# First feed-forward matrix by seven half-size products, second matrix in chunks, in a hybrid encoder layer

## Chip, cores and metric

The kernel runs on one core of one Trainium2 chip. The metric is the device time of one launch in microseconds (us), median of the runs. The engines of a core are named as in the profile: PE (TensorE, matrix products; PEld is its loading of weights), DVE (VectorE), ACT (ScalarE), POOL (GpSimd), SP (SyncE, which issues most DMAs).

## The reference, cut to what matters

One layer, 512 tokens and 16 meta tokens, 1024 features, float32. The layer is feed forward, mixer, feed forward, each with a norm ahead and behind it:

```
def swiglu(x, wi, wo):                 # wi: 1024 x 5632, wo: 2816 x 1024
    a, b = split(x @ wi, 2)
    return (silu(a) * b) @ wo

h = h + 0.5 * rmsnorm(swiglu(rmsnorm(h, n[0]), ffn1_wi, ffn1_wo), n[1])
h = h + rmsnorm(hybrid_mixer(rmsnorm(h, n[2]), ...), n[3])
h = h + 0.5 * rmsnorm(swiglu(rmsnorm(h, n[4]), ffn2_wi, ffn2_wo), n[5])
return h[16:]
```

The first feed forward has all 528 token columns, the second only the 512 that are returned. The mixer is not touched by the change.

## The kernel before

**Layout.** Features lie on partitions, tokens on columns: `hT` is [128, 8, 528]. A weight matrix is stored as tiles of 128 output features, each [128, 8, 128] for 1024 inputs (512 KB). `wi` has 44 of them: tiles 0 to 21 are `a`, tiles 22 to 43 are `b`, so that tile m and tile 22+m make a pair (`KF` is 22). `wo` has 8 tiles (`KD`), each of 22 inner tiles.

**Exact products.** Every float32 operand is split into two float32r parts of 12 significand bits, `h` and `l`: ACT casts (L219, L224), DVE subtracts what the cast kept (L220, L225). `mm` (L227) makes a product from three passes: h by h, h by l, l by h. `load` (L212) stages a weight tile in `ws` (2 buffers), splits it to `wh` and `wl` (3 buffers each), and asks for a priority that lies 150 instructions ahead (`AHEAD`). Only PE's order is written by hand; the other engines' orders come from a scheduler that goes by priority, which otherwise is the order in the program. Each engine then runs its own queue in order.

**A unit** (`unit`, L243) is one tile of `wi` against all columns: 8 inner tiles by 3 passes. For the first feed forward the 528 columns go as two halves of 264 in two PSUM banks, 48 matrix instructions (`ALLC`); for the second as one bank of 512, 24 instructions (`REAL`). There are two PSUM pools of four banks each, `pb` (`big`) and `pd` (`dnp`).

**Feed forward** (`ffn`, L518). The norm ahead of it is applied late: the products use h times the gain, and the factor `rx` (one per token, written by the reciprocal at L276) multiplies what comes out (`scaled`, L502; L539, L542 for the first pairs). Per pair: two units, scale, silu, multiply (L526), split into `gh` and `gl`, which hold all 22 inner tiles. The first three units come with the pre-stage (`start` L334, or `edge` L375); the next three run while `rx` is made. Then the second matrix: for output tile m = 0 to 6 all 22 inner tiles are summed in PSUM (L557 to L563), and `evict_y` (L305) copies the result to `y`, squares it and sums the squares in `acc`. Tile 7 is the tail.

**Tail, edge and finish.** The last output tiles are made for one half of the columns and then for the other (`part`, L324), so that the norm of the first half can start under the products of the second. `edge` (L375) goes from one stage to the next, `finish` (L431) writes the output: DVE multiplies and adds 8 tiles of the first half (L461, L462), PE transposes, and after the last product ACT squares it (L489) and DVE makes the last rows (L499). For the feed forwards the tail is one tile with 22 inner tiles; for the mixer it is three tiles with 8.

Of the kernel before, what the change touches and what calls it, by code (L numbers as in the profile page):

```python
# [29 lines left out]
AHEAD = 150  # L30
XW = 5.0
# [23 lines left out]
# columns of the packed constants  # L55
# [45 lines left out]
class Cols:  # L101
    """Token columns of a stage, in two halves; joined: both fit one PSUM bank."""
# [17 lines left out]
class Tensor:  # L120
    """The tensor engine's instructions, with a sum of their length that orders the side work."""
# [22 lines left out]
class K:  # L144
# [43 lines left out]
    # side work goes between the large products; it yields how far on its next part goes  # L188
# [22 lines left out]
    # weights: staged as stored, then split into two parts of 12 significand bits  # L211
# [93 lines left out]
    def evict_y(self, ya, m, ps, gain=None, table=KD - 2):  # L305
        """ps: (half, what the products of tile m gave for it)"""
        y, acc = ya
        ACT, V = self.nc.scalar, self.nc.vector
        for i, p in ps:
            w = acc[i].shape[1]  # L310
            if gain is None:
                ACT.copy(y[i][:, m, :w], p)
            else:
                ACT.activation(y[i][:, m, :w], p, AF.Copy, scale=self.gains[:, gain, m:m + 1])
            if m == 0:
                ACT.activation(acc[i], p, AF.Square)
            else:
                sq = self.t(self.tp, "sy", [P, HN], F32, 1)[:, :w]
                ACT.activation(sq, p, AF.Square)  # L319
                V.tensor_tensor(acc[i], acc[i], sq, op=ALU.add)  # L320
        if m == table:
# [12 lines left out]
    def start(self, xT, gpre, srcs):  # L334
        """the first norm and tiles: everything arrives in the order of need"""
# [28 lines left out]
        # warm-up products while the first loads arrive  # L364
# [10 lines left out]
    def edge(self, C, hT, ya, gpost, gpre, tail, switch, nxt):  # L375
# [18 lines left out]
        tiles, tx, tc = tail()  # L394
        for t in tiles:
            self.evict_y(ya, t[0], [(0, self.part(t, tx, tc[0], W))], table=tiles[0][0] - 1)
# [12 lines left out]
        for t in tiles:  # L409
            self.evict_y(ya, t[0], [(1, self.part(t, tx, tc[1], W, lambda: next(e, None)))], table=-1)  # L410
# [20 lines left out]
    def finish(self, hT, ya, tail, out):  # L431
        """the last norm and residual; the second half of the tokens goes by tokens"""
# [5 lines left out]
        (tile,), tx, tc = tail()  # L438
        last = tile[0]
# [8 lines left out]
        self.evict_y(ya, last, [(0, self.part(tile, tx, tc[0], W))], 5, -1)  # L448
# [36 lines left out]
        p = self.part(tile, tx, tc[1], W, lambda: next(e, None))  # L485
# [3 lines left out]
        ACT.activation(sq[:, :W], p, AF.Square)  # L489
        ACT.activation(y[1][:, last, :W], p, AF.Copy, scale=self.gains[:, 5, last:last + 1])  # L490
# [20 lines left out]
    def open_ffn(self):  # L511
        ctx = ExitStack()
        gp = ctx.enter_context(self.tc.tile_pool(name=self.uid("gp"), bufs=1))
        self.gp = gp
        self.t3 = lambda: self.t(gp, "t3", [P, 530], F32, 3)
        return ctx

    def ffn(self, pre, wi, wo, C, gain=None):  # L518
        nc = self.nc
        x, os = pre  # L520
        gh = self.t(self.gp, "gh", [P, KF, L], F32R)
        gl = self.t(self.gp, "gl", [P, KF, L], F32R)
        u = C.u

        def pair(m, a, b):
            nc.vector.tensor_tensor(a[:, u], a[:, u], b[:, u], op=ALU.mult)  # L526
            self.split(gh[:, m, u], gl[:, m, u], a[:, u])

        def silu(a):
            nc.scalar.activation(a[:, u], a[:, u], AF.Silu)  # L530

        y = self.ytile().rearrange("p k c -> p (k c)")
        a, b, a1 = (y[:, i * L:(i + 1) * L] for i in range(3))
# [4 lines left out]
        for t in (a, b):  # L538
            nc.vector.tensor_tensor(t[:, u], t[:, u], self.rx[:, u], op=ALU.mult)  # L539
        silu(a)  # L540
        pair(0, a, b)
        nc.vector.tensor_tensor(a1[:, u], a1[:, u], self.rx[:, u], op=ALU.mult)  # L542
        silu(a1)
        b = self.t3()
        self.scaled(b, o)
        pair(1, a1, b)
        for m in range(2, KF):
            a = self.t3()
            self.scaled(a, o2 if m == 2 else self.unit(wi[m], x, C))
            silu(a)  # L550
            b = self.t3()
            self.scaled(b, o3 if m == 2 else self.unit(wi[KF + m], x, C))
            pair(m, a, b)
        ya = self.start_y(C)
        chunks = [(k0, min(8, KF - k0)) for k0 in range(0, KF, 8)]
        g = (gh, gl)
        for m in range(KD - 1):  # L557
            o = self.outs(C)
            for k0, n in chunks:
                w = self.load(wo[m][:, k0:k0 + n], n)  # L560
                for k in range(n):
                    self.mm(o.full, w, g, k, k0 + k, k0 + k == 0, k0 + k == KF - 1)
            self.evict_y(ya, m, [(i, p) for i, (p, _) in enumerate(o.half)], gain)  # L563

        def tail():
            ws = [(self.load(wo[KD - 1][:, k0:k0 + n], n), n, k0) for k0, n in chunks]
            return [(KD - 1, [(w, k, k0 + k) for w, n, k0 in ws for k in range(n)])], g, C.halves
        return ya, tail

# [18 lines left out]
    def mixer(self, pre, hT):  # L588
# [100 lines left out]
        def tail():  # L689
            ws = [(m, self.load(A["wout"][m])) for m in range(KD - NT, KD)]  # L690
            return [(m, [(w, k, k) for k in range(KD)]) for m, w in ws], (mh, ml), CS.halves
# [39 lines left out]
    def fold(self, q, o, fh, fl):  # L731
# [13 lines left out]
        def fold():  # L745
# [18 lines left out]
            # token L - k for k = 1 .. L/2 - 1  # L764
# [30 lines left out]
    # per-token scalars of both directions, [token, head, direction, tile]; tile 4: meta tokens  # L795
# [6 lines left out]
    def ab(self, ab):  # L802
# [23 lines left out]
        # softplus(a) = max(a, 0) + 2 atanh(e / (2 + e)), e = exp(-|a|)  # L826
# [5 lines left out]
        # beta = 1 / (1 + exp(-x))  # L832
# [50 lines left out]
    # short conv and silu of one head's q, k or v  # L883
# [8 lines left out]
    # token-major copies and l2norm  # L892
# [38 lines left out]
    # both heads' k: l2norm, token-major and back  # L931
# [41 lines left out]
    def rsqrt(self, dst, src, scale=1.0):  # L973
        """1 / sqrt(src * scale + eps) of a few columns: a first value from the exponent, then Newton's steps"""
# [11 lines left out]
    # chunk matrices and the scan of a pair of heads, both directions  # L986
    def dn_core(self, st, slack):
# [6 lines left out]
        # [token, head * 2 + direction, tile]  # L994
# [11 lines left out]
        # exponents gc_i - gc_j, masked  # L1006
# [36 lines left out]
        # inverses of the 32 x 32 diagonal blocks, one block a partition  # L1043
# [55 lines left out]
        # the blocks beside the diagonal  # L1099
# [25 lines left out]
        # scan  # L1125
# [80 lines left out]
    # gated norm of one head's output, back to channel-major, in place  # L1206
# [30 lines left out]
def body(tc, A):  # L1237
    nc = tc.nc
    with ExitStack() as ctx:
# [15 lines left out]
        ya, tail = k.ffn(pre, wi, wo, ALLC)  # L1255
# [14 lines left out]
        ya, tail = k.ffn(pre, wi, wo, REAL, 5)  # L1270
# [55 lines left out]
```

## Time and profile before

| | |
|---|---|
| median of 3 runs (lowest, highest) | 1327.59 us (1327.44, 1327.77) |
| span of the profiled execution | 1325.0 us |
| median less that span: what lies around it | 2.6 us |
| mean granted PE clock | 0.999 |
| PE instructions of the wi units of the two feed forwards, from the code | 2112 and 1056 |

The profiled execution's own time is not listed apart from its span; it is taken as the span and the 2.6 us. A row of the grouped view gives line, engine, operation, tiles and shapes, count, then busy us and mean ns of one, then the idle time of the engine before these instructions and what ended it. A row of the timeline gives start, length, engine, line, and in brackets the idle time before it with its releaser. In the chain of waits a piece is start, length, what.

### The profile page before, as it was taken

Reading aid. Unit: us, or ns where it says so; the run is one execution under the profiler, and the core shown is the slowest. Engines: PE = TensorE matmul, PEld = TensorE weight load, DVE = VectorE, ACT = ScalarE, POOL = GpSimd, SP = SyncE. Lnnn points to the kernel's source line nnn. Section 1 sums busy time; section 2 is a strip of 40 time slices with the busy share of each in tenths; the row PEclk is TensorE's granted clock in tenths of the full one; section 3 lists DMA queues with packets and bytes.
Section 4 is the critical chain, followed back from the end, with each engine's and each line's share of the span. In section 5 each row is a group of like instructions: output and inputs, shape, how many; then the busy total and the mean of one; then the engine's idle time right before and its main releaser. Section 6 shows DMA issues by size and latency. Waiting matters only on the chain.

```text
span 1325.0 us, 20942 instructions
## 1 busy us (share of the span) xinstructions
PE 1311.5 (99%) x8575; PEld 1159.8 (88%) x8575; DVE 741.3 (56%) x1524; ACT 492.3 (37%) x911; POOL 4.7 (0%) x12
## 2 busy tenths in 40 slices
PE   9999999999999999999999999999999999999998
PEld 9999999999999988778987777888978888888887
DVE  6644444422239888758788578564774444442223
ACT  7322222222235452344633434334552222222222
POOL 0000000000000000000000000000000000000000
PEclk9999999999999999999999999999999999999999
DMA  6322323333225222322221222235133332333332
GB/s 196 96 83 93 95 81 96 91 84 94 88 85 189 85 72 89 107 70 70 75 65 60 70 64 66 87 102 175 49 112 95 95 96 96 95 92 95 96 90 74
DMA packets 49844, 123.05 MB, mean 93 GB/s; under 512 B 13388, under 2 KB 17612, under 8 KB 49748
## 3 DMA queue, kind: packets, MB, share of 16 engines
q1 hardware_dynamic: 44660, 120.14, 29.2%
q10 hardware_dynamic: 5088, 1.57, 0.5%
q8 instruction: 67, 1.10, 0.3%
q14 instruction: 29, 0.24, 0.1%
HBM read 116.42 MB, written 5.28 MB: 92 GB/s over the span
## 4 chain that ended last, share of the span: by engine, by line
PE 95%; DVE 2%; ACT 1%; DMA 0%; SPq 0%; issue 0%; DVEq 0%; ACTq 0%
PE pb L137 86%; PE pd L137 8%; PE pd L141 1%; DVE s L386 1%; DVE x L391 1%; DVE wl L220 0%; DVE h L388 0%; ACT wh L219 0%; DMA h<-in_xT 0%; ACT O L1170 0%; DVE acc L288 0%; DVE x L499 0%; PE pb L141 0%; SPq L352 0%; ACT vp L1179 0%
## 5 line engine op out<-in xcount | busy, mean ns | idle before, releaser
L137 PE MATMUL pb<-x,wh 128*128 128x264 f32 (+3 forms) x3296 | 720.5, 325 | 3.5 <-DVE x L391 1.4
L137 PEld LDWEIGHTS pb<-x,wh 128*128 128x128 f32 x3296 | 513.8, 188 | 59.8 <-issue 4.6
L137 PE MATMUL pb<-x,wl 128*128 128x264 f32 (+3 forms) x1648 | 450.2, 323 | 1.1 <-DVE wl L220 1.0
L219 ACT CAST wh<-ws 128x1024 fp32r<-128x1024 f32 (+2 forms) x222 | 219.2, 988 | 613.3 <-PE pb L137 589.0
L220 DVE TENSOR_TENSOR wl<-ws,wh 128x1024 fp32r<-128x1024 f32 (+2 forms) x222 | 253.8, 1144 | 197.4 <-ACT wh L219 196.8
L137 PEld LDWEIGHTS pb<-x,wl 128*128 128x128 f32 x1648 | 276.5, 188 | 26.8 <-DVE wl L220 1.9
L504 DVE TENSOR_TENSOR t<-pb,rx 128x264 f32<-128x264 f32 (+2 forms) x144 | 67.7, 499 | 228.8 <-PE pb L137 228.8
L137 PE MATMUL pb<-gh,wh 128*128 128x264 f32 (+2 forms) x550 | 149.0, 316 | 0.0
L137 PE MATMUL pb<-gh,wl 128*128 128x264 f32 (+2 forms) x550 | 148.0, 315 | 0.0
L137 PE MATMUL pb<-gl,wh 128*128 128x264 f32 (+2 forms) x550 | 147.6, 314 | 0.0
L137 PEld LDWEIGHTS pb<-gl,wh 128*128 128x128 f32 x550 | 93.2, 188 | 6.9
L137 PEld LDWEIGHTS pb<-gh,wh 128*128 128x128 f32 x550 | 93.2, 188 | 6.5
L137 PEld LDWEIGHTS pb<-gh,wl 128*128 128x128 f32 x550 | 93.1, 188 | 6.6
L137 PE MATMUL pb<-y,wh 128*128 128x512 f32 x192 | 61.7, 402 | 0.0
L137 PEld LDWEIGHTS pb<-y,wh 128*128 128x128 f32 x192 | 34.4, 188 | 8.5 <-issue 2.2
L137 PE MATMUL pb<-y,wl 128*128 128x512 f32 x96 | 37.5, 391 | 0.0
L224 ACT CAST gh<-t 128x528 fp32r<-128x528 f32 (+1 forms) x40 | 25.1, 628 | 31.1 <-DVE t L526 31.1
L700 DVE TENSOR_TENSOR t<-pb,rx 128x512 f32<-128x512 f32 x24 | 16.6, 690 | 32.0 <-PE pb L137 32.0
L137 PE MATMUL pd<-x,wh 128*128 128x264 f32 (+2 forms) x176 | 33.3, 294 | 0.0
L1179 ACT ACTIVATE vp<-pd,be 64x128 f32<-64x128 f32 x64 | 23.2, 363 | 21.1 <-PE pd L137 19.8
L320 DVE TENSOR_TENSOR acc<-acc,sy 128x256 f32<-128x256 f32 (+1 forms) x41 | 17.4, 424 | 24.0 <-ACT sy L319 24.0
L526 DVE TENSOR_TENSOR t<-t,t 128x528 f32<-128x528 f32 (+1 forms) x40 | 28.0, 699 | 3.8
(261 smaller groups left out, 1113.1 us busy)
## 6 DMA issues: line engine op xcount, KB each, us to landing
ws<-in_wi SPq DMA_DIRECT2D x85, 512.0 KB, 3.5
ws<-in_wo SPq DMA_DIRECT2D x32, 512.0 KB, 3.4
ws<-in_win SPq DMA_DIRECT2D x32, 512.0 KB, 3.5
ws<-in_wg SPq DMA_DIRECT2D x24, 512.0 KB, 3.4
ws<-in_wo SPq DMA_DIRECT2D x16, 384.0 KB, 3.2
ws<-in_wout SPq DMA_DIRECT2D x8, 512.0 KB, 3.4
keep<-h SPq DMA_DIRECT2D x1, 2048.0 KB, 7.9
ws<-in_wsc SPq DMA_DIRECT2D x8, 256.0 KB, 2.7
```

Of the source, the lines that this page charges most:

```text
L137: return self.e.matmul(out, lhsT, rhs, **kw)
L141: return self.e.transpose(*a)
L219: nc.scalar.copy(h[:, :nk], st[:, :nk])
L220: nc.vector.tensor_tensor(l[:, :nk], st[:, :nk], h[:, :nk].bitcast(F32), op=ALU.subtract)
L224: self.nc.scalar.copy(h, src)
L320: V.tensor_tensor(acc[i], acc[i], sq, op=ALU.add)
L386: V.scalar_tensor_tensor(t, ya[0][i][:, k, :W], self.gains[:, gpost, k:k + 1], r[:, c], op0=ALU.mult, op1=ALU.mult)
L391: V.scalar_tensor_tensor(x[1][:, k, c], hT[:, k, c], g, x[0][:, k, c].bitcast(F32), op0=ALU.mult, op1=ALU.subtract)
L504: self.nc.vector.tensor_tensor(dst[:, c.start + off:c.stop + off], p, self.rx[:, c], op=ALU.mult)
L526: nc.vector.tensor_tensor(a[:, u], a[:, u], b[:, u], op=ALU.mult)
L700: nc.vector.tensor_tensor(g, o.full[0][0], self.rx[:, NM:], op=ALU.mult)
L1179: ACT.activation(v1[X, hd], b[X, hd * P:(hd + 1) * P], AF.Copy, scale=beta[X, hd, t:t + 1])
```

## The change

Of each feed forward the first four pairs stay as they are. Pairs 4 to 21 are made from seven half-size products in place of eight (Winograd's form of Strassen's scheme): the columns of the input are halved into two halves of tokens, the inner features into two halves of four tiles, and the two weight tiles of the pair are the two output halves.

**Inputs** (`seven`). The normed input (h by gain by `rx`) is computed, 16 DVE instructions; from its four blocks come seven operands, four of them sums, each [128, 4, 264] and each split into `h` and `l`. Three are made in `seven`, between pair 2 and pair 3, and four in `rest`, after pair 4 has begun; those lie in the buffers of the old input `x`.

**Weights** (`pair_load`). Seven operands of half a tile come from one pair: two as stored, two sums by a DMA that adds to what another DMA has written (issued from POOL, `accum_op`), two sums by DVE, the last also by DVE. Four staging buffers `wf`, three used by a pair.

**Products.** 12 instructions each (4 inner tiles, 3 passes, 264 or 256 columns). Sums of products are kept by copying a PSUM bank to another with ACT and going on to accumulate there, with a product of another bank in between. The order on PE, n the next pair and p the one before: 1n, 7p, 3p, 5n, 4p, 2n, 6n.

**Second matrix in chunks.** Pairs 0 to 5, 6 to 13 and 14 to 21 each fill a `gh`, `gl` of at most 8 inner tiles, and after each chunk all output tiles are summed over that chunk, and added to `y` by DVE. The last two steps of a chunk's last pair (products 7, 3, 4) lie between the first two output tiles. The tail now is three output tiles with 8 inner tiles, added to `y`.

```
+    def seven(self, hT, C, gpre):
+        xn = [self.ytile() for _ in range(2)]
+        for k in range(KD):
+            for i, c in enumerate(C.halves):
+                V.scalar_tensor_tensor(xn[i][:, k, :W], hT[:, k, c], self.gains[:, gpre, k:k + 1], self.rx[:, c],
+                                       op0=ALU.mult, op1=ALU.mult)
...
+        put(1, h3[:, 0, :, :W], l3[:, 0, :, :W], A11)
+        V.tensor_tensor(s5, A21, A22, op=ALU.subtract)
+        put(5, h3[:, 1, :, :W], l3[:, 1, :, :W], s5)
+        put(2, h3[:, 2, :, :W], l3[:, 2, :, :W], A12)
+        def rest():
...
+    def pair_load(self, w1, w2):
+        with self.tc.high_priority(AHEAD2):
+            fa, fb, fc = (self.t(self.gp, "wf", [P, KD, P], F32, 4) for _ in range(3))
+            fd = self.t(self.wp, "ws", [P, KD, P], F32, 2)
+            lo, hi = slice(0, 4), slice(4, 8)
+            nc.sync.dma_start(fa[:, lo], w1[:, lo])
+            nc.sync.dma_start(fa[:, hi], w1[:, lo])
+            nc.gpsimd.dma_start(fa[:, hi], w2[:, lo], accum_op=ALU.add)
+            nc.sync.dma_start(fb[:, lo], w1[:, hi])
+            nc.sync.dma_start(fc[:, hi], w2[:, hi])
+            nc.sync.dma_start(fc[:, lo], w2[:, hi])
+            nc.gpsimd.dma_start(fc[:, lo], w2[:, lo], accum_op=ALU.add)
...
+            put(fa, 1, 5)
+            V.tensor_tensor(fb[:, hi], fa[:, hi], fc[:, hi], op=ALU.add)
+            put(fb, 2, 6)
+            put(fc, 7, 3)
+            V.tensor_tensor(fd[:, lo], fb[:, hi], fb[:, lo], op=ALU.add)
+            put(fd, 4, None, 4, "w4", self.gp, 1)
...
+        def begin(m):
+            product(1, st, st.b0, True)
+            ACT.copy(st.b1, st.b0)
+        def five(st):
+            product(5, st, b4, True)
+            ACT.copy(st.p5, b4)
+        def two(st):
+            product(2, st, st.b0, False)
+            ACT.activation(st.ev[:, 0, :W], st.b0, AF.Silu)
+        def six(st):
+            product(6, st, st.b1, False)
+            ACT.copy(st.b2, st.b1)
+        def seven(st):
+            product(7, st, st.b2, False)
+            V.tensor_tensor(st.ev[:, 1, W:2 * W], st.b2, st.p5, op=ALU.add)
+            product(3, st, st.b1, False)
+            V.scalar_tensor_tensor(st.ev[:, 1, :W], st.b1, -1.0, st.p5, op0=ALU.mult, op1=ALU.subtract)
+        def four(st, g, m):
+            product(4, st, st.b2, False)
+            ACT.activation(st.ev[:, 0, W:2 * W], st.b2, AF.Silu, scale=-1.0)
+            pair(g, m, st.ev[:, 0, :2 * W], st.ev[:, 1, :2 * W])
...
+            for m in ms:
+                nxt = begin(m)
+                if st:
+                    seven(st)
+                five(nxt)
+                if st:
+                    four(st, gc, st.m - k0)
+                two(nxt)
+                if m == 4:
+                    rest()
+                six(nxt)
+                st = nxt
+            for m in range(KD - 3 if final else KD):
...
 def evict_y(...):
-            if gain is None:
+            if more:
+                V.tensor_tensor(y[i][:, m, :w], y[i][:, m, :w], p, op=ALU.add)
+                p = y[i][:, m, :w]
+            elif gain is None:
```

In `finish` the last product is added to `y` by DVE before ACT squares it; `edge` and `finish` go over the three tail tiles. To open the three banks that are filled by copies, three single PE instructions are issued once in each feed forward.

More of the change, by code (lines that the diff above doesn't have):

```diff
@@ L303, in start_y, with evict_y @@
         return y, acc
[L305 removed]
+    def evict_y(self, ya, m, ps, gain=None, table=KD - 2, more=False):
         y, acc = ya
@@ L320, in evict_y @@
                 V.tensor_tensor(acc[i], acc[i], sq, op=ALU.add)
+            if more and gain is not None:
+                ACT.activation(p, p, AF.Copy, scale=self.gains[:, gain, m:m + 1])
         if m == table:
@@ L437, in finish @@
         y, acc = ya
-        (tile,), tx, tc = tail()
-        last = tile[0]
+        tiles, tx, tc, more = tail()
+        last = tiles[-1][0]
         outA = out[:, :KD * W].rearrange("p (k c) -> p k c", k=KD)
@@ L447, in finish @@
         yT = []
-        self.evict_y(ya, last, [(0, self.part(tile, tx, tc[0], W))], 5, -1)
+        for t in tiles:
+            self.evict_y(ya, t[0], [(0, self.part(t, tx, tc[0], W))], 5, -1, more)
         bs = []
@@ L484, in finish @@
         e = early()
-        p = self.part(tile, tx, tc[1], W, lambda: next(e, None))
+        for t in tiles[:-1]:
+            self.evict_y(ya, t[0], [(1, self.part(t, tx, tc[1], W, lambda: next(e, None)))], 5, -1, more)
+        p = self.part(tiles[-1], tx, tc[1], W, lambda: next(e, None))
         for _ in e:
@@ L520, in ffn, with gtiles, pair @@
+    def ffn(self, pre, wi, wo, C, hT, gpre, gain=None):
+        nc = self.nc
+        V, ACT, T = nc.vector, nc.scalar, self.T
         x, os = pre
-        gh = self.t(self.gp, "gh", [P, KF, L], F32R)
-        gl = self.t(self.gp, "gl", [P, KF, L], F32R)
         u = C.u
-        def pair(m, a, b):
-            nc.vector.tensor_tensor(a[:, u], a[:, u], b[:, u], op=ALU.mult)
-            self.split(gh[:, m, u], gl[:, m, u], a[:, u])
+        W = C.halves[0].stop - C.halves[0].start
+        chunks = [range(0, 6), range(6, 14), range(14, KF)]
+        def gtiles():
+            return tuple(self.t(self.gp, n, [P, KD, L], F32R) for n in ("gh", "gl"))
+        def pair(g, m, a, b):
+            V.tensor_tensor(a, a, b, op=ALU.mult)
+            self.split(g[0][:, m, u], g[1][:, m, u], a)
@@ L547, in ffn @@
[L547 to L563, printed above, removed]
+        self.scaled(b1, o)
@@ new lines, in ffn @@
+        pair(g, 1, a1[:, u], b1[:, u])
+        e = self.ev()
+        self.scaled(e[:, 0], o2)
+        silu(e[:, 0])
+        self.scaled(e[:, 1], o3)
+        pair(g, 2, e[:, 0, u], e[:, 1, u])
+        X, rest = self.seven(hT, C, gpre)
+        e = self.ev()
+        self.scaled(e[:, 0], self.unit(wi[3], x, C))
+        silu(e[:, 0])
+        self.scaled(e[:, 1], self.unit(wi[KF + 3], x, C))
+        pair(g, 3, e[:, 0, u], e[:, 1, u])
+        seeded = [self.dnp()[:, :W] for _ in range(3)]
@@ L565, in tail @@
         def tail():
-            ws = [(self.load(wo[KD - 1][:, k0:k0 + n], n), n, k0) for k0, n in chunks]
-            return [(KD - 1, [(w, k, k0 + k) for w, n, k0 in ws for k in range(n)])], g, C.halves
+            ws = [(m, self.load(wo[m][:, k0:k0 + n], n)) for m in range(KD - 3, KD)]
+            return [(m, [(w, k, k) for k in range(n)]) for m, w in ws], gc, C.halves, True
         return ya, tail
```

142 lines of the change are left out of this document (121 added, 21 removed).

## Prediction

> **What bounds the kernel now.** I read the page first: PE is busy for 99% of the span and makes 95% of the chain that ended last. So time is won by fewer or shorter PE instructions, and lost by every hole that PE gets.
>
> ```profile
> span 1325.0 us, 20942 instructions
> ...
> PE 1311.5 (99%) x8575; PEld 1159.8 (88%) x8575; DVE 741.3 (56%) x1524; ACT 492.3 (37%) x911; POOL 4.7 (0%) x12
> ...
> PE 95%; DVE 2%; ACT 1%; DMA 0%; SPq 0%; issue 0%; DVEq 0%; ACTq 0%
> ```
>
> A busy PE says nothing of its pace, so I took that from the timeline. The ACT cast of a weight tile starts when a unit ends and frees its buffer. Two rows with one other unit's cast between them are two units apart, which is one pair: 11.74 us in the first feed forward (96 instructions of 264 columns, 0.1223 us each), 11.12 us in the second (48 of 512, 0.2317 us).
>
> ```profile
> 60.23 1.05 ACT L219 CAST wh<-ws 128x1024 fp32r<-128x1024 f32 x1 [3.54 <-PE pb L137]
> ...
> 71.97 1.05 ACT L219 CAST wh<-ws 128x1024 fp32r<-128x1024 f32 x1 [3.54 <-PE pb L137]
> ...
> 1041.01 1.05 ACT L219 CAST wh<-ws 128x1024 fp32r<-128x1024 f32 x1 [3.23 <-PE pb L137]
> ...
> 1052.13 1.05 ACT L219 CAST wh<-ws 128x1024 fp32r<-128x1024 f32 x1 [3.23 <-PE pb L137]
> ```
>
> The second feed forward will issue 256 columns at a time. The tail shows that width: from the first product of the first half to the first of the second are 66 instructions, 7.76 us, 0.1176 us each.
>
> ```profile
> 1297.86 0.28 PE L137 MATMUL pb<-gh,wh 128*128 128x256 f32 x1
> ...
> 1305.62 0.29 PE L137 MATMUL pb<-gh,wh 128*128 128x256 f32 x1
> ```
>
> **What PE is relieved of.** A changed pair has 7 products of 12 instructions, 84. First feed forward: 84 x 0.1223 = 10.27 us in place of 11.74, a product being 1.47 us; 18 pairs save 26.4 us. Second: 84 x 0.1176 = 9.88 in place of 11.12, a product 1.41 us; 18 pairs save 22.3. Together 48.7 us, less six seed instructions (0.7): 48.0. The second matrix keeps its number of instructions; chunking costs PE nothing by itself.
>
> **Steady pairs: does the rest keep up?** The grouped view by shape gives the prices.
>
> ```profile
> L220 DVE TENSOR_TENSOR wl<-ws,wh 128x1024 fp32r<-128x1024 f32 x182 | 222.1, 1221 | 156.5 <-ACT wh L219 155.9
> L219 ACT CAST wh<-ws 128x1024 fp32r<-128x1024 f32 x182 | 191.0, 1050 | 505.6 <-PE pb L137 489.8 <-issue 10.9 <-DMA ws<-in_wout 1.8
> ...
> L504 DVE TENSOR_TENSOR t<-pb,rx 128x264 f32<-128x264 f32 x98 | 37.9, 426 | 120.4 <-PE pb L137 120.4
> ...
> L220 DVE TENSOR_TENSOR wl<-ws,wh 128x512 fp32r<-128x512 f32 x24 | 16.4, 682 | 1.5 <-ACT wh L219 1.4
> ...
> L219 ACT CAST wh<-ws 128x512 fp32r<-128x512 f32 x24 | 14.9, 620 | 54.5 <-PE pb L137 46.0 <-issue 6.5 <-ACT EZ L1124 1.9
> ...
> L526 DVE TENSOR_TENSOR t<-t,t 128x528 f32<-128x528 f32 x20 | 14.2, 708 | 1.9
> L225 DVE TENSOR_TENSOR gl<-t,gh 128x528 fp32r<-128x528 f32 x20 | 14.0, 702 | 1.4 <-ACT gh L224 1.4
> ...
> L312 ACT COPY y<-pb 128x264 f32<-128x264 f32 x16 | 6.0, 377 | 4.1 <-PE pb L137 4.1
> ```
>
> DVE per changed pair: three splits of 1024 (3.66), one of 512 (0.68), two sums of 512 (as the split, 1.36), two evictions of 264 (0.85), multiply and split (1.41): 8.0 us of 10.27, or of 9.88. ACT: 3.15 + 0.62, three copies and two silus at 0.38 (1.9), one cast of 528 at about 0.6: 6.3 us. Both fit, DVE at about 80%. The order on PE leaves slack at each hand-over but one. The weights of product 1 are freed after product 5 and wanted three products later: 4.4 us for a cast and a split (2.3). DVE's reading of bank b2 after product 7 has two products (2.9 us). The tight one is product 7: six ends, ACT copies b1 to b2 (0.38), and only product 1 (1.47, or 1.41) covers it; the buffer of fb falls free at that same moment, so a cast of 1.05 with its raised priority can stand in front: 1.05 + 0.38 is just the cover. I take 0.1 us a pair, ends 0 and 0.3: 34 pairs (17 behind another in each feed forward), 3 us, 0 to 10.
>
> That raised priority does go ahead of what PE waits for is seen in the edge to the mixer: in the chain of waits a weight split for a later unit (1.14 us in a full queue) lies between steps that PE's next product needs. This view gives the pace of a full DVE queue, too: 1.14 for a split, 0.40 for a three-operand instruction of 264.
>
> ```profile
> 395.86 0.89 DVE x L391 x2
> 396.75 1.14 DVE wl L220
> ...
> 398.57 0.80 DVE s L386 x2
> ```
>
> **The start of the seven products.** Here I expect the largest loss. The operands need `rx`, and DVE has it only at 36.3 and 973.9 us; PE would reach pair 4 two units after unit KF+2. DVE, which now ends the first three pairs in this stretch, must make the operands in it, too.
>
> ```profile
> 32.82 3.47 DVE L276 RECIPROCAL rx<-rx 128x264 f32<-128x264 f32 x2 [0.57 <-ACT rx L275]
> ...
> 36.90 5.87 PE pd L137 x48
> ...
> 36.20:47.10 10.90, 10.90 (x91) 10.90 (x90) 9.65 (x18) 5.54 (x8) 0.00 (x0) 1.00 0.23 61
> ...
> 970.55 3.36 DVE L276 RECIPROCAL rx<-rx 128x256 f32<-128x256 f32 x2
> ...
> 974.43 5.56 PE pd L137 x24
> ...
> 973.90:984.46 10.56, 10.56 (x47) 8.55 (x46) 9.75 (x15) 6.88 (x9) 0.00 (x0) 1.00 0.24 81
> ```
>
> The second of the two window rows' columns that matter is DVE's: 9.65 and 9.75 us busy with pairs 0 to 2 and two splits. To this comes, up to the operand of product 3 of pair 4: 16 instructions for the normed input at 0.40 (6.4), six operand splits of 1056 at 1.17 (7.0), four sums at 1.2 (4.8), pair 4's three weight splits and a sum (4.0), four evictions of pair 3 at 0.34 (1.4), the next pair's first split (1.1). Sum 34.4, so to 70.7; with what stands before it in program order and could have waited (pair 3's multiply and split, the last weight sum and split, the next pair's second: 4.1) to 74.8. PE would be there at 42.77 + 2 x 5.87 + 6 x 1.47 = 63.3. The hole is 7.4 to 11.5 us, and more where DVE waits for ACT's casts between. In the second: 9.75 + 24.1 = 33.9, to 1007.8 or 1011.9; PE 979.99 + 2 x 5.56 + 6 x 1.41 = 999.6; hole 8.2 to 12.3. I take 10 each, 20 in all, ends 14 and 26. It does not lie in one piece: some 2 us before product 1, 2 before 5, 4 to 5 before 6 (whose sum is only begun in `rest`, behind pair 3), the rest after.
>
> **The borders of the chunks**, three in each feed forward. The first `wo` tile's buffer is freed after product 5 and wanted after 2 and 6 (2.9 us for 2.3 of cast and split); the same holds for the second pair of a chunk; output tile 2 waits in the first feed forward for the eviction of tile 0, behind a cast. Each is within 1 us of its cover. Six borders at 1 us: 6, ends 2 and 12. DVE's adds to `y` (0.43) lie under products of 4.4 to 5.9 us a tile.
>
> **The tails.** DVE adds ahead of ACT's squares, for two more tiles. In `finish` DVE is full from 1310.3 and PE's last transposes now wait for tiles that are added behind this; the last product passes DVE (0.4) before ACT. In the edge DVE is on the chain already, and gets some 1.5 us more. Together 2 us, ends 0.5 and 4.
>
> ```profile
> 1310.31 0.76 DVE L461 TENSOR_TENSOR s<-y,r 128x256 f32<-128x256 f32 x2 [1.92 <-ACT r L272]
> ...
> 1317.70 0.38 ACT L489 ACTIVATE sy<-pb 128x256 f32<-128x256 f32 x1 [2.22 <-PE pb L137]
> ```
>
> **Sum**: 48.0 - 20 - 3 - 6 - 2 = 17.0 us. The span goes to 1308.0, and with the 2.6 us around it the time to 1310.6; the runs before stand within 0.2 us of that base. By the terms' own ends it is 1327.6 - 48.0 + 16.5 = 1296 to 1327.6 - 48.0 + 52 = 1332.
>
> **Rival 1, slower: the summed weights come late.** No row shows a DMA from POOL, let alone one that adds. Buffer fa of pair n+2 is fc of pair n, which can be split when product 3 of n-1 is done; counted from product 1 of pair n that is 4.4 + 2.3, with queueing 8 us. The plain loads land at 11, the adding DMA starts then, takes L, and cast and split (2.3) must be over when product 1 of n+2 is due, at 20.5 (19.8 in the second): L may be 7.2 (6.5). The rows bound L by a plain load of 256 KB below and by the 2 MB write above:
>
> ```profile
> ws<-in_wsc SPq DMA_DIRECT2D x8, 256.0 KB, 2.7
> ...
> keep<-h SPq DMA_DIRECT2D x1, 2048.0 KB, 7.9
> ```
>
> I take L near 4, as the nearer of the two. Above 6.9 on the mean each us costs a us in the third and later pairs of each long chunk, 6 x 2 x 2 = 24 pairs. The gain of 17 is gone at L = 7.6; at the upper end, 7.9, it costs 24 and gives 1335, at 8.2 it gives 1342. Also behind such a late sum stands DVE: its sum fb waits for fa in order, and evictions behind it.
>
> The Trainium skill, DMA: Bandwidth & Descriptors, section "Anatomy of one DMA — SWDGE (gpsimd) path", gives 2.0 us and the bytes over 436 GB/s for a plain DMA on this path, which I work out as an estimate of 2.6 us for 256 KB; by it this rival would not happen. No run here shows such a DMA.
>
> **Rival 2: the start is mostly covered.** If the scheduler lets pair 3 and later splits stand back and sums are early, the holes come to their lower ends of 7.4 and 8.2, steady pairs lose nothing and borders 2: 1327.6 - 48.0 + 15.6 + 2 + 1 = 1298. For it: DVE is idle at every unit in the steady part. Against: it is full in just this stretch.
>
> **Rival 3: a hole slows PE's clock.** At the end PE does nothing from 1319.0, and the granted clock (the column behind POOL) goes from 1.00 to 0.50 some 3.9 us later.
>
> ```profile
> 1319.00:1320.00 1.00, 0.01 (x1) 0.00 (x0) 0.94 (x4) 0.04 (x1) 0.00 (x0) 1.00 0.00 0
> ...
> 1322.00:1323.00 1.00, 0.00 (x0) 0.00 (x0) 0.00 (x0) 0.00 (x0) 0.00 (x0) 0.95 1.00 377
> 1323.00:1324.00 1.00, 0.00 (x0) 0.00 (x0) 0.00 (x0) 0.00 (x0) 0.00 (x0) 0.50 0.54 207
> ```
>
> The hole before product 6 is put at 4 to 5 us. If the clock then stays at half for as long as it took to fall, 3.9 us at half pace lose 2 us each: 1315.
> The Trainium skill, TensorE: Matmul & The Clock Gate, section "What's actually happening", states this rule: half clock after an idle window of about 3.4 us, full clock after as long a busy one. The end of this trace agrees (3.9 us); by the rule each hole over one window would cost an estimated 1.7 us.
>
> **How the numbers follow.** My forecast as summed has 0.50, rival 3 0.12, rival 2 0.13, rival 1 and its like, above 1330, 0.19; 0.06 is for the terms' far ends meeting the time before. No change, for which 0.2% (2.7 us) is what a measurement can tell, is 1324.9 to 1330.2. Faster: 0.50 + 0.12 + 0.13 = 0.75, less 0.02 for the forecast's upper end, 0.73; same 0.07; slower 0.20. The likeliest alone reaches from 1300 to 1324. The range goes down to rival 2 with its lower tail at 1295, up into rival 1 at 1337.
>
> **What would show it.** Right: wi pairs 10.3 and 9.9 us apart in the steady part; PE waiting for the operand splits (`h3`, `l3`, `x`) at some 54 to 76 and again in the second start, 7 to 12 us each; DVE near 80% in the pairs; landing of the adding DMAs under 7 us. Wrong: PE waits for DMAs or `wl` in most pairs (rival 1); a hole at the start under 4 us; pairs at 11 us or more with no releaser but ACT or DVE; a granted clock under 1 there (rival 3).

## The result, and the profile after

The changed kernel takes 1390.3 us (median; 1382.4 to 1397.5) against 1327.7 before: 1.047 times as long, with a 95% interval of 1.043 to 1.051. The forecast was 1310.6 us. Three lines of the changed kernel's page, its span, its engines and the chain that ended last by engine:

```profile
span 1395.7 us, 22738 instructions
...
PE 1309.1 (94%) x9019; PEld 1182.7 (85%) x9019; DVE 892.0 (64%) x1750; ACT 604.4 (43%) x1155; POOL 67.1 (5%) x84
...
PE 73%; DVE 11%; DMA 10%; ACT 3%; issue 3%; SPq 0%; DVEq 0%; ACTq 0%; POOLq 0%
```

PE's share of the chain fell from 95% to 73%. DVE and DMA, which were 2% and 0%, now carry a fifth of it. PE also looks almost as busy as before (1309 us), though it has fewer columns to compute. To see why, the table cuts each whole span into windows of one microsecond. The sum of (1 - PE busy) is PE's idle time; the sum of PE busy x (1 - granted clock) is an estimate of what a slow clock cost; the rest of the span is work at full clock.

| kernel | span | PE idle | lost to the clock | work at full clock |
|---|---|---|---|---|
| before | 1325.0 | 13.6 | 0.0 | 1311.4 |
| changed | 1395.7 | 86.6 | 32.4 | 1276.7 |
| chunks alone, no seven products | 1332.8 | 15.7 | 3.4 | 1313.7 |
| changed, without the adding DMAs | 1332.9 | 44.5 | 14.6 | 1273.8 |
| changed, five staging buffers | 1352.9 | 66.4 | 10.4 | 1276.1 |
| changed, half-size staging buffers | 1325.9 | 41.2 | 11.4 | 1273.3 |
| the same, products from pair 5 | 1308.8 | 27.6 | 6.1 | 1275.1 |

The work did fall, by 35 us. PE's waiting rose by 73 us, and the clock took 32 more. The changed kernel's waits (in total, times, longest) name where PE stands:

```profile
PE pd L138 <- ACT pd L696: 31.7, 20, 1.6
PE pb L138 <- DVE wl L226: 14.5, 12, 2.0
PE pb L138 <- DVE l L226: 7.1, 2, 6.1
PE pd L138 <- ACT x L225: 6.7, 2, 3.8
PE pb L138 <- DVE ev L515: 6.4, 1, 6.4
```

The last three rows are the two starts. The first two come in the pairs, 20 and 12 times: L696 is the copy of b1 to b2 that product 7 adds to, `wl` at L226 a split of product 1's weights. Neither engine is full (DVE 64%), so both are late for another reason. The chain of waits through one steady pair of the second feed forward shows it (start, length, what):

```profile
1114.87 1.24 DVE wl L226
1116.11 0.02 issue
1116.12 5.43 DMA wf<-in_wi
...
1121.65 0.70 DVE wf L604
...
1128.05 1.24 DVE wl L226
1129.29 0.02 issue
1129.31 4.67 DMA wf<-in_wi
...
1134.07 0.70 DVE wf L604
```

Read it as a ring. The split of fb ends at 1116.11 and frees a staging buffer. The next pair's fc is loaded into that buffer, issued 0.01 us later. DVE's sum fb (L604) needs fc, and DVE stood idle for it until 1121.65. Behind the sum stand, in DVE's order, a split, the other sum, two more splits (one of half size) and the gate multiply. ScalarE takes its cast of the gate only after that, and next the cast of fb, whose split (1128.05) frees the buffer for the next load at 1129.31. Once round took 13.19 us. (Between sum and cast the chain names fc's adding DMA, landing at 1127.23; but the cast had begun by then, as the next rows show, so I go by the queue.) ScalarE's timeline of the same pair:

```profile
1126.45 0.62 ACT L225 CAST gh<-ev 128x512 fp32r<-128x512 f32 x1 [3.50 <-DVE ev L623]
1126.98 1.04 ACT L225 CAST wh<-wf 128x1024 fp32r<-128x1024 f32 x1
1127.93 0.36 ACT L696 COPY pd<-pd 128x256 f32<-128x256 f32 x1
```

ACT was idle for 3.50 us behind the gate multiply; the copy that product 7 waits for is the third in that queue. So PE's largest wait bears the name of a copy of 0.36 us, while what is late is a load, far upstream.

That round shows one way in which the sum comes late. There is a second, and it is the more frequent one. The sum also needs the half of fa that is loaded and then added to. DVE waited at the sum for 72.4 us, in 29 times. The first of these rows, from the list of who waited for fa's adding DMA (L590), and the second, from the same list for fc's load (L592), divide them:

```profile
  DVE wf L604: 45.4, 17
```

```profile
  DVE wf L604: 27.0, 12
```

A round through fa, from the SP, POOL, DVE and again SP timelines (L589 is the plain load, L590 the adding DMA into the same half):

```profile
1148.68 0.43 SPq L589 DMA_DIRECT2D wf<-in_wi  x1
```

```profile
1153.69 0.86 POOL L590 DMA_DIRECT2D wf<-in_wi  x1 [5.24 <-DMA wf<-in_wi]
```

```profile
1158.69 0.69 DVE L604 TENSOR_TENSOR wf<-wf,wf 128x512 f32<-128x512 f32 x1 [2.00 <-DMA wf<-in_wi]
1159.31 1.22 DVE L226 TENSOR_TENSOR wl<-wf,wh 128x1024 fp32r<-128x1024 f32 x1
```

```profile
1160.93 0.42 SPq L589 DMA_DIRECT2D wf<-in_wi  x1
```

The adding DMA goes out when the plain load has landed, and the sum 10.01 us after the plain load was issued. Behind the sum DVE makes a split of fc (it ends at 1160.53), which frees the buffer into which the next fa is loaded. Once round took 12.25 us, of which 2.24 us are not the series of plain load and adding DMA.

The holes cost twice. Three windows of 3.4 us of the changed kernel (length, then busy PE, PEld, DVE, ACT, POOL; the granted clock is the number behind POOL):

```profile
1252.90:1256.30 3.40, 1.45 (x10) 1.25 (x10) 2.87 (x4) 1.07 (x4) 0.00 (x0) 0.96 0.80 209
1256.30:1259.70 3.40, 2.01 (x9) 2.01 (x10) 1.92 (x2) 1.61 (x4) 0.86 (x1) 0.50 0.36 92
1259.70:1263.10 3.40, 3.40 (x19) 3.40 (x18) 0.42 (x1) 0.09 (x1) 0.00 (x0) 0.54 0.73 200
```

PE was busy for 1.45 of 3.40 us in the first, and the two windows after it ran at 0.50 and 0.54.

### The profile page after: what moved, and what is told of

It reads as the page before. It is cut to its first block, busy times and chain, and to the rows that moved or that the text cites. A ratio compares the mean times of both kernels' runs of the same rounds, so it can differ in the third digit from the quotient of the medians.

```text
span 1395.7 us, 22738 instructions
## 1 busy us (share of the span) xinstructions
PE 1309.1 (94%) x9019; PEld 1182.7 (85%) x9019; DVE 892.0 (64%) x1750; ACT 604.4 (43%) x1155; POOL 67.1 (5%) x84
## 4 chain that ended last, share of the span: by engine, by line
PE 73%; DVE 11%; DMA 10%; ACT 3%; issue 3%; SPq 0%; DVEq 0%; ACTq 0%; POOLq 0%
PE pb L138 55%; PE pd L138 17%; DMA wf<-in_wi 9%; DVE wl L226 3%; ACT wh L225 2%; PE pd L142 1%; DVE ev L623 1%; DVE ws L607 1%; DVE wl L221 1%; DVE y L545 1%; ACT wh L220 1%; DVE w4l L226 1%; DVE x L397 1%; DVE rx L277 0%; DVE wf L604 0%
## 5 line engine op out<-in xcount | busy, mean ns | idle before, releaser
L138 PE MATMUL pb<-x,wh 128*128 128x264 f32 (+3 forms) x1568 | 353.6, 329 | 4.7 <-DVE x L397 2.3
L138 PEld LDWEIGHTS pb<-x,wh 128*128 128x128 f32 x1568 | 246.0, 189 | 35.7 <-issue 4.6
L138 PE MATMUL pd<-x,wh 128*128 128x264 f32 (+2 forms) x1040 | 215.8, 307 | 41.2 <-ACT pd L696 31.7
L138 PE MATMUL pb<-x,wl 128*128 128x264 f32 (+3 forms) x784 | 219.6, 325 | 1.1 <-DVE wl L221 1.0
L138 PEld LDWEIGHTS pd<-x,wh 128*128 128x128 f32 x1040 | 176.1, 207 | 48.5 <-ACT pd L696 35.9
L226 DVE TENSOR_TENSOR wl<-wf,wh 128x1024 fp32r<-128x1024 f32 x108 | 132.0, 1222 | 35.3 <-ACT wh L225 34.9
L138 PE MATMUL pd<-x,wl 128*128 128x264 f32 (+2 forms) x520 | 153.0, 302 | 0.0
L138 PEld LDWEIGHTS pb<-x,wl 128*128 128x128 f32 x784 | 133.3, 189 | 14.4 <-DVE wl L221 1.7
L138 PE MATMUL pb<-h,wl 128*128 128x264 f32 (+1 forms) x432 | 126.5, 293 | 14.7 <-DVE wl L226 14.5
L138 PE MATMUL pb<-l,wh 128*128 128x264 f32 (+1 forms) x432 | 125.6, 291 | 7.1 <-DVE l L226 7.1
```

Of the source, the lines that this page charges most:

```text
L138: return self.e.matmul(out, lhsT, rhs, **kw)
L226: self.nc.vector.tensor_tensor(l, src, h.bitcast(F32), op=ALU.subtract)
```

## The experiments

Theory 1 was the first ring, through fc. Its rivals were the adding DMA itself, ScalarE's order, DVE's order alone, the chunks, and the operands at the start. The kernel before ran beside every one of them, at 1327.4 to 1327.6 us.

**Which part of the change costs.** One kernel keeps the chunks and computes all pairs by ordinary tiles. Another leaves out the adding DMAs:

```
# a_buf5:     fa, fb, fc = (... F32, 4) -> (... F32, 5)
# b_noadd:    nc.sync.dma_start(fa[:, hi], w1[:, lo])                 -> ... w2[:, lo]
#             nc.gpsimd.dma_start(fa[:, hi], w2[:, lo], accum_op=ADD) -> gone; fc[:, lo] likewise
# p_poolsum:  V.tensor_tensor(fb[:, hi] ...), (fd[:, lo] ...) -> nc.gpsimd.tensor_tensor
# e_chunks:   pairs 4 to 21 by self.unit(), pair() as pairs 0 to 3; no begin, five, two, six, leave
```

Chunks alone: 

> The second matrix in chunks with all pairs by ordinary tiles, no seven products. Forecast of the prediction: chunk borders 6 and, with ordinary tails, up to 2: 1327.6 + 6 = 1334 (1329 to 1342). Theory 1 (all the loss stands in the seven products' pairs): the same, 1329 to 1340, and the granted clock stays near 1.00. Rival D (the chunks bring the loss, by the holes at their borders): 1355 or more.

Measured: 1334.5 us, 1.0056 (1.0039 to 1.0073): 7 us over before. The chunks are not the cause. The 7 us hold the borders (here between ordinary pairs) and the longer tails, for which the forecast had 6 and 2.

Without the adding DMAs: 

> The two adding DMAs are left out: fa's and fc's halves are loaded once, so that two of the four weight sums are not made and the output is another one; the other work is the same. Theory 1 (late buffers, VectorE in order): the load that ends the wait at the sum is then the plain one of fc, issued as late as before, so the period stays above 11.5 us and the time at 1360 to 1385 us. Rival A (the adding DMA itself is late by its 4 to 5 us): the waits at the sum vanish and the time falls to 1315 to 1340. Rival B (ScalarE's order): 1375 or more.

Measured: 1334.2, 1.005 (1.004 to 1.007). Rival A's number, not theory 1's: 56 of the 63 us vanish with the adding DMAs, although fc's buffer is freed and loaded in the same order as before. The ring through fa is gone, for there is no series any more. Is the ring through fc wrong, then? The DVE and SP timelines of that kernel say it is only shorter (L591 is the load of fc's half here, L602 the sum):

```profile
1112.35 1.22 DVE L226 TENSOR_TENSOR wl<-wf,wh 128x1024 fp32r<-128x1024 f32 x1 [0.26 <-ACT wh L225]
...
1116.30 0.69 DVE L602 TENSOR_TENSOR wf<-wf,wf 128x512 f32<-128x512 f32 x1
...
1122.70 1.22 DVE L226 TENSOR_TENSOR wl<-wf,wh 128x1024 fp32r<-128x1024 f32 x1 [0.26 <-ACT wh L225]
```

```profile
1113.60 0.33 SPq L591 DMA_DIRECT2D wf<-in_wi  x1
...
1123.95 0.33 SPq L591 DMA_DIRECT2D wf<-in_wi  x1
```

Split, load, sum and split again stand in the same order. From load to sum are 2.70 us here and were 5.53 with the adding DMAs; once round is 10.35 us and was 13.19. The rest of the ring is the same to 0.01 us (7.65 and 7.66; in the changed kernel's next round 7.65). The round of 13.19 is one of the slowest: fc's load landed after 3.5 us in the median of the changed kernel (5.4 at most) and after 2.7 here. So a pair takes the longest of PE's work, 7.7 us plus the time until fc is there, and 2.2 us plus the series into fa. The page's issues in the changed kernel and in this one (KB each, median us to landing) agree:

```profile
wf<-in_wi SPq DMA_DIRECT2D x180, 256.0 KB, 3.9
wf<-in_wi POOLq DMA_DIRECT2D x72, 256.0 KB, 4.2
```

```profile
wf<-in_wi SPq DMA_DIRECT2D x180, 256.0 KB, 2.9
```

In the ring through fc the adding DMA's own landing has no place; there it counts by what the plain loads beside it take. In the ring through fa it stands itself. Theory 1's ring is real, but it was the lesser part: its forecast for this run (that fc's load would take as long without the adding DMAs) fell, and rival A's held.

Five buffers: 

> Five staging buffers for the summed weights instead of four, nothing else. Theory 1 (a staging buffer comes free only with the split of the pair before; the load into it lands about 5 us later; VectorE stands at its sum fb until then, and behind the sum stand the splits, the gate multiply, and by way of ScalarE's casts the copy that product 7 waits for): the load of fc is issued some 4 us earlier, VectorE's 72.4 us of waiting for loads at the sum fall below 25, a pair of the second matrix comes down from 12.5-13 us to 10.3-11, and with fewer holes the half-clock windows become few: 1325 to 1350 us. Rival A (the adding DMA behind its plain load is what is late, however early the buffer): the sum goes on waiting, 1370 or more. Rival B (ScalarE's order alone, the cast of fb ahead of the copy): 1375 or more.

Measured: 1355.0, 1.021 (1.020 to 1.023), a little above theory 1's range. PE's waits for the copy are gone, but DVE's waiting at the sum did not fall: 102.1 us. The ring through fa is left, and now ends 73.5 us of these waits, in 19 of 31 times. SP, POOL, DVE and PE timelines of this kernel, in that order:

```profile
1104.91 0.42 SPq L589 DMA_DIRECT2D wf<-in_wi  x1
...
1117.26 0.42 SPq L589 DMA_DIRECT2D wf<-in_wi  x1
```

```profile
1109.30 0.86 POOL L590 DMA_DIRECT2D wf<-in_wi  x1 [7.67 <-DVE ev L623]
```

```profile
1115.02 0.69 DVE L604 TENSOR_TENSOR wf<-wf,wf 128x512 f32<-128x512 f32 x1 [4.40 <-DMA wf<-in_wi]
1115.63 1.22 DVE L226 TENSOR_TENSOR wl<-wf,wh 128x1024 fp32r<-128x1024 f32 x1
```

```profile
1117.84 0.51 PE L138 MATMUL pd<-x,w4h 128*128 128x256 f32 x2 [1.99 <-DVE ev L700]
```

The plain load of fa goes out at 1104.91, the adding DMA 4.39 us later, the sum 5.72 us after that, its split ends at 1116.85, and the loads of the next pair go out at once: 12.35 us round. Plain load and adding DMA in series are 10.1 us of it, and the rest is 2.24 us, as in the changed kernel.

Sums on GpSimd: 

> The sums fb and fd on GpSimd instead of VectorE. Rival C (nothing is late but what stands behind the waiting sum in VectorE's order: splits of the other weights and the gate multiply): VectorE no longer stands, 1320 to 1345 us. Theory 1: the buffers come free as late as before, and the sum itself may take longer than VectorE's 0.70 us; the gate multiply is no longer held, the weights of products 1 and 7 still are: 1350 to 1400.

Measured: 1366.9, 1.030 (1.028 to 1.031). In theory 1's range, not in rival C's. But a GpSimd sum took 1.66 or 1.96 us in the mean where DVE's takes 0.69, and in GpSimd's queue the adding DMAs now stand behind the waiting sums, so the run does not test rival C cleanly. PE's waits for the copy remain (39.4 us).

**Order of single steps.**

```
# c_copy:    with self.tc.high_priority(400): ACT.copy(st.b2, st.b1)
# f_buf5ev:  five buffers, and with self.tc.high_priority(400): around L700 and L702
# d_order:   X, rest = self.seven(hT, C, gpre) moved behind pair 3's evictions, multiply and split
```

> ScalarE's copy into the bank of product 7 is put ahead of the cast of fb. Rival B (ScalarE's order alone: PE's longest wait, 31.7 us in 20 times before product 7, ends with that copy): the wait goes and nothing follows, 1340 to 1355 us. Theory 2, after the first runs (the plain load and the adding DMA behind it, in series some 9 to 10 us with the wait for the buffer on top, are what is late, and the copy is only where it comes out): the wait moves to product 1's or product 5's weights, 1378 to 1395.

Measured: 1382.2, 1.041 (1.038 to 1.044); the interval touches that of the change itself. The wait before product 7 went from 31.7 to 25.8 us. But the run hardly tests rival B: in its trace the copy stands ahead of the cast of fb in only 4 of the 30 pairs that have both, and the order of the other 26 is as it was. In those four PE still waited 0.7 to 1.3 us before product 7, and the next sums came 11.6 to 12.8 us apart. What speaks against rival B is the run without the adding DMAs, and the one with half-size buffers further down: there the copy still stands behind the cast, and the waits of 1.6 us before product 7 are gone.

> Five staging buffers, and VectorE's two evictions of product 7 and product 3 put ahead of the sum fb. With five buffers alone (1355.0) PE waits 25.6 us in 20 times for the first of these evictions, which stands behind the sum while the sum waits for the adding DMA. Theory 2a (VectorE's order decides what a late sum costs): these waits go, a pair takes 10.3 to 10.8 us, 1328 to 1338 us. Theory 2b (the series of plain load and adding DMA, 10.1 us from issue to landing in that trace, paces the pairs itself): the wait moves to product 5's or 6's weights, 1346 to 1356.

Measured: 1355.5, 1.021 (1.020 to 1.023), the same as five buffers alone. It tells nothing of 2a against 2b: in its trace both evictions still stand behind the sum, so the priority did not move them.

> The operands X1 to X7 of the seven products are asked for after pair 3's eviction, gate multiply and split instead of before. Theory on the start (its first idle piece, 6.4 us in the first feed-forward, is a PSUM bank whose eviction stands behind the operand work on VectorE, not the operand): that piece goes, the rest of the start's 11.4 and 11.7 us stays in part, and one or two half-clock windows at each start go: 1365 to 1380 us against 1390. Rival (the operands are the price, and asking later only moves the hole behind pair 3): 1385 to 1400.

Measured: 1391.4, 1.049 (1.046 to 1.052). The wait for the bank (L515) is gone and that for operand splits (`l`, L226) grew from 7.1 to 16.3 us. The hole only moved; the theory on the start fell and its rival held.

**The sums in other ways.**

```
# g_poolterm: ga, gb = two half-size buffers; plain loads of w2[:, lo] into them;
#             nc.gpsimd.tensor_tensor(fa[:, hi], fa[:, hi], ga); (fc[:, lo], fc[:, lo], gb)
# i_dvesum:   the same with V.tensor_tensor
# q_traffic:  as b_noadd, with the plain loads of w2[:, lo] into ga, gb, which nobody reads
```

> The two adding DMAs are replaced by plain loads into half-size buffers of their own and by GpSimd's additions; all sums are made. Theory 2 (the adding DMA's place in the series is the loss): as without the adding DMAs, 1330 to 1345 us. Rival E (without the adding DMAs it was quicker only for the 0.25 MB that each of them moves less, or GpSimd's additions are as slow as the DMA): 1360 or more.

Measured: 1428.5, 1.076 (1.074 to 1.078). A miss: GpSimd's two additions took 1.67 and 2.15 us, and DVE's sum into fd beside them 1.49 in place of 0.69.

> The two adding DMAs are replaced by plain loads into half-size buffers and by additions on VectorE, 0.69 us each; all sums are made. Theory 2: no series of load and adding DMA, VectorE at 9.4 of a pair's 10.3 us: 1335 to 1350 us. Rival G (VectorE becomes the bound, as GpSimd's additions of 1.7 to 2.2 us did to the pairs in the run before): 1360 or more.

Measured: 1370.7, 1.034 (1.032 to 1.037). A miss too, and an instructive one: there is no adding DMA, and DVE still waits 67.0 us for loads at the sum. Whatever lengthens a ring brings the loss back. Here it is the one through fc, in one round 3.10 us from load to sum and 8.27 us for the rest, where without the adding DMAs it was 2.70 and 7.65: DVE's additions stand in it, and the loads are slower.

> The kernel without the adding DMAs (1334.2), with two plain loads of 256 KB more in each pair, from GpSimd's queue, into buffers that nobody reads; the two sums are not made, as there. If the adding DMAs cost by their traffic (they slow the plain loads that the sum waits for): 1365 or more. If they cost by their series (the sum waits for a DMA that had to wait for another): 1333 to 1342 us.

Measured: 1343.4, 1.013 (1.011 to 1.015), just above the second forecast. Its ring, by the loads of fc on SP and the sum on DVE (L605):

```profile
1110.50 0.33 SPq L593 DMA_DIRECT2D wf<-in_wi  x1
...
1121.44 0.33 SPq L593 DMA_DIRECT2D wf<-in_wi  x1
```

```profile
1113.78 0.69 DVE L605 TENSOR_TENSOR wf<-wf,wf 128x512 f32<-128x512 f32 x1 [0.68 <-DMA wf<-in_wi]
```

3.28 us from load to sum, 10.94 round, so 7.66 beside the load once more. Two plain loads more per pair, of the same size as the adding DMAs, cost 9 us of the 56. fc's load lands after 3.1 us in the median, between the 2.7 without them and the 3.5 beside adding DMAs. So traffic is the smaller part, and most of the loss goes with the adding itself, as the ring through fa has it. How the other 47 us divide between that ring and the slower load of fc was not taken apart; five buffers, which leave mainly the ring through fa, take off 35 of the 63.

**Breaking the ring.** Half-size buffers let each load wait only for its own half, in the room of five whole buffers:

```
ah, cl = (self.t(self.gp, "wa", [P, 4, P], F32, 4) for _ in range(2))   # w1+w2 halves: plain load + adding DMA
al, bl, ch, bh = (self.t(self.gp, "wf", [P, 4, P], F32, 6) for _ in range(4))
for n, q, s in zip((a, b), (lo, hi), f):     # each split in two halves
    self.split(h[:, q], l[:, q], s)
# j_halves: loads and adding DMAs of ah, cl first; n_lateorder: in the changed kernel's order
```

> Half-size staging buffers, ten of them (as much room as five whole ones): four for the two halves that are added to, so that their plain load and their adding DMA can go out a whole pair ahead, ahead of the other loads; each split is made in two halves. Theory 2 (the adding DMA costs because its series, some 10 us, begins less than a pair before its sum is needed): the waits at the sum fall below 25 us, pairs take 10.4 to 10.9 us, 1328 to 1342 us. Rival F (the adding DMAs slow the other loads, or the splits that hang on them, wherever they stand): 1350 or more.

Measured: 1329.1, 1.001 (1.000 to 1.002): as fast as before, with all four sums made and the adding DMAs in place. No wait of PE in the steady pairs is left. Two pairs of each feed forward, by the eviction after product 3:

```profile
271.96 0.43 DVE L702 SCALAR_TENSOR_TENSOR ev<-pd,p 128x264 f32<-128x264 f32 x1 [1.01 <-PE pd L138]
282.36 0.43 DVE L702 SCALAR_TENSOR_TENSOR ev<-pd,p 128x264 f32<-128x264 f32 x1 [1.01 <-PE pd L138]
...
1121.88 0.42 DVE L702 SCALAR_TENSOR_TENSOR ev<-pd,p 128x256 f32<-128x256 f32 x1 [0.99 <-PE pd L138]
1132.06 0.42 DVE L702 SCALAR_TENSOR_TENSOR ev<-pd,p 128x256 f32<-128x256 f32 x1 [1.01 <-PE pd L138]
```

10.40 and 10.18 us a pair, PE's own pace; the changed kernel had 10.2 to 16.6. The adding DMAs land no sooner than before (4.7 us in the median), but now nothing waits for them.

> The ten half-size buffers of the run with 1329.1, but the loads issued in the changed kernel's order, the adding DMAs and their plain loads among the others. If the room that half-size buffers give is what counts (each load waits only for its own half): 1327 to 1336 us. If the order counts (the adding series has to go out ahead of the loads that wait for buffers): 1345 to 1360, as with five whole buffers.

Measured: 1330.5, 1.002 (1.001 to 1.004). So the order of issue does not matter, and what the half-size buffers give does.

**The clock and the start.**

```
# h_filler: ahead of seven(st): 12 x T.matmul(nxt.bank[:, W:2*W-16], X[1][0][:, 0, :P], X[1][0][:, 0, :W-16], start=True, stop=True)
# l_start5: d_order, pair 4 by ordinary tiles, rest() at pair 5, s5 in a buffer of its own
# m_best:   j_halves and l_start5 (the difference s5 made again in rest() in place of its own buffer)
```

> Twelve dummy matmuls of 0.11 us, 1.3 us in all, ahead of product 7 of each pair, into unused columns of a bank; nothing reads them. They lie in the hole of 1.6 us that PE has there. Theory on the clock (a window of 3.4 us in which PE was busy less than about half is followed by one at half clock, which costs some 32 us of the 1390): fewer such windows, granted clock 0.98 or more in the mean, 1362 to 1378 us. Rival (only the idle time costs, the clock follows something else): the dummies are hidden or add, 1388 to 1420.

Measured: 1427.2, 1.075 (1.073 to 1.078). Dummies in the bank of product 1 change what that bank holds, so the output is another one; the other work is the same. Lost to the clock were 22.8 us in place of 32.4, but the time rose by 37. PE's idle time hardly fell (80.8 us in place of 86.6), and DVE's waiting at the sum doubled, from 72.4 to 144.0 us. A likely reason, not tried by itself, is that PE is a part of the ring through fc (the cast of fb follows product 6), so that work put in a hole makes the ring longer and the hole comes again. The price of the clock by itself was not isolated; the 32 us rest on the windows alone.

> The operands of the seven products asked for after pair 3, as in the order run (1391.4), and pair 4 by ordinary tiles, so that 11.7 or 11.1 us of PE's work stand between the operands and their first use; the products begin with pair 5. Theory (the operand work is the start's price and one pair more covers most of it): the start's idle 23 us fall below 10, with the half-clock windows behind them, less the seven products' gain on two pairs of which nothing was left: 1362 to 1378. Rival (evictions and splits stand behind the operand work wherever it is put): 1385 or more.

Measured: 1361.9, 1.027 (1.025 to 1.029). The first start in the changed kernel and in this one, by windows:

```profile
50.00:75.00 25.00, 14.90 (x90) 14.17 (x90) 21.36 (x31) 11.04 (x14) 1.73 (x2) 0.73 0.34 89
```

```profile
50.00:75.00 25.00, 22.34 (x184) 22.13 (x183) 23.23 (x37) 13.32 (x17) 0.86 (x1) 1.00 0.38 105
```

PE is busy for 22.34 us in place of 14.90, and the clock stays at 1.00. DVE has as much to do as before, but PE has a pair's work meanwhile. PE's waits at the two starts are 9.9 us in all, where the run with the order alone had 26.0; the theory had said below 10.

> The half-size staging buffers with the adding DMAs a pair ahead (1329.1) and the later start (operands asked for after pair 3, the products from pair 5) in one kernel; X6's difference is made again, one VectorE instruction more. If the two causes are separate, as theory 2 and the theory on the start have it, their gains add: 1329.1 - (1391.4 - 1361.9) = 1300, at least the half of the start's idle 24.6 us and half-clock loss 11.4 us: 1296 to 1312 us, and so faster than before. If the start's gain in that run came from the late staging (pairs that wait less after another start): 1322 to 1330.

Measured: 1311.7 us, 0.988 (0.987 to 0.990): faster than both kernels, by 1.2% and 5.7%. It lies in the forecast's range by 0.3 us and far from the rival's. So the start is a cause of its own, though it brought 17 us here and not 29; why the gains add only in part was not looked into. Its page:

```profile
span 1308.8 us, 22842 instructions
...
PE 1281.1 (98%) x8995; PEld 1157.9 (88%) x8995; DVE 901.9 (69%) x1848; ACT 615.8 (47%) x1245; POOL 63.6 (5%) x80
...
PE 90%; DVE 6%; ACT 2%; DMA 1%; issue 1%; SPq 0%; DVEq 0%; ACTq 0%
```

## Why the prediction was wrong

**The step that failed** is the steady pairs: "I take 0.1 us a pair, ends 0 and 0.3: 34 pairs ..., 3 us". With the half-size buffers no such wait is left, all sums are made, and the time is 61 us shorter; so these waits, with the clock that follows them, cost about 61. I had added up each engine's busy time, found 8.0 of 10.27 us on DVE, and looked for slack at each hand-over singly. What sets the pair is two rings of hand-overs, each with its slack used up by the one before, and both longer than PE's 10.2 to 10.4 us: plain load and adding DMA into fa, 10 us in series, with 2.2 us of sum and split; and the load of fc, 3 to 5 us, with 7.7 us of sums, casts and splits. Product 7, where "a cast of 1.05 with its raised priority can stand in front", was seen right as the place where the loss comes out, but not as its cause. With the rings broken this hand-over by itself is small. ACT and PE of the kernel with half-size buffers:

```profile
1118.32 0.36 ACT L696 COPY pd<-pd 128x256 f32<-128x256 f32 x1
```

```profile
1118.49 0.28 PE L138 MATMUL pb<-h,wl 128*128 128x256 f32 x1
1118.74 0.50 PE L138 MATMUL pd<-x,wh 128*128 128x256 f32 x2
1119.08 0.28 PE L138 MATMUL pd<-x,wl 128*128 128x256 f32 x1
```

The copy ends at 1118.68, and three steps of PE take 0.59 us where three others take 0.36: 0.23 us a pair, inside the ends of 0 and 0.3.

**Rival 1** had the link that ended 17 of the 29 waits: the series into the buffer that fc frees. It allowed the adding DMA 7.2 us and took 4. Into fa it landed after 5.0 us in the median (6.7 at most), so by that reckoning nothing was to be lost. Two things in it failed. It gave the series until product 1 two pairs on, with the buffer freed by PE's schedule. But the sum that needs fa stands in DVE's order ahead of the split that frees the next buffer, so a round must fit into one pair, which leaves about 8 us (10.2 less 2.2) for both transfers. And it had 3 us for the plain load and 4 for the adding DMA, together 7, where the round above has 10. (A plain DMA of this size from GpSimd's queue, for which the prediction gave an estimate of 2.6 us, landed after 3.4 us in the median in the run with two plain loads more.) It also did not follow the plain load of fc through the buffer that fb frees, which has about 2.7 us before it delays PE. "Also behind such a late sum stands DVE" was the sentence to work out; I only wrote it.

**Start**: 20 forecast, ends 14 and 26. In the changed kernel PE waited 11.4 and 11.7 us at the two starts, 23.1 in all and inside the ends, and some 9.8 us went to the clock on top (windows from 45 to 110 and from 960 to 1060). The placing was off: 6.4 us of the first hole come in one piece before product 1, whose bank's eviction stood behind operand work on DVE.

**Chunk borders and tails**: 6 and 2 forecast, 7 measured together with the chunks alone. **Relief of PE**: 48.0 forecast. From the chunks alone to the kernel without adding DMAs the work falls by 39.9. Undisturbed pairs took 10.40 and 10.18 us, not 10.27 and 9.88; times 18 each that is 7.7 of the 8.1 missing. I took the rate from one long run of products, which has no hand-over like the one into product 7; its 0.23 us are most of the 0.30 missing in a pair of the second feed forward.

**Rival 3**, the clock, was a real effect, with 0.12 and 2 us a hole far too small. I asked for a hole of a whole window and looked for one at the start only. The steady pairs' holes, of up to 1.6 and 2.0 us, were enough where one or two of them took about half of a window.

## What to carry to other kernels

When a stage is pipelined through few buffers, follow one buffer all the way round: freed, loaded, added to, summed, cast, split, freed. That time, not any engine's busy share, is the floor of the stage, and a queue that runs in order puts every other step of the engine into the ring. Count a transfer that adds as the whole series (plain load, issue, addition), and from the step that frees its buffer, not from PE's schedule; ask also what it does to the loads beside it. And if the ring is too long, finer buffers may do more for the same room than more of them (1329 us against 1355 here).

## What the hardware showed that was not expected

An adding DMA of 256 KB landed 4.2 us after its issue in the median (5.0 into fa, 4.1 into fc). Beside the adding DMAs fc's plain load landed after 3.5 us in the median, without them after 2.7, and with as many plain loads from GpSimd's queue in their place after 3.1. GpSimd added 128x512 floats in 1.7 to 2.2 us in the mean, DVE in 0.69, and in 1.49 beside GpSimd's additions. The granted clock fell to half after a window of 3.4 us in which PE had been busy for 1.45 us. The Trainium skill, TensorE: Matmul & The Clock Gate, section "What's actually happening", states half clock after an idle window; by these rows the window need not be idle.
